# Key tiles cleared first, ScalarE's first operations chained, and the first projections reordered by kinds of parts

## The chip, the cores and the metric

The kernel runs on one core of one Trainium2 chip. The time is device microseconds (us) of that core for one execution, and smaller is better. A core has five engines with a queue of instructions each, worked off in order: PE (TensorE, matrix products and transposes), ACT (ScalarE), DVE (VectorE), POOL (GpSimd) and SP (SyncE, which here only issues DMAs). An instruction waits at the head of its queue until what it depends on is done, and everything behind it on that engine waits too.

## The reference

One layer of a hybrid decoder over 1024 tokens with 16 meta tokens put in front (1040 rows, model width 1024), all in float32:

```
u = RMSNorm(h)
z = u @ W_in -> [q | k | v | x_rec | y_rec]          (512 + 128 + 128 + 512 + 512 columns)
group A: causal depthwise conv(4) -> RG-LRU on x_rec, gated by GeLU(y_rec)
group B: sliding-window (128) attention, 8 heads on 2 KV heads, one sink per head
h += RMSNorm(concat(B_out, A_out) @ W_out)
h += RMSNorm(W2 relu(W1 RMSNorm(h))^2)
```

The output is h without the 16 meta rows. What the change touches lies in the first three lines: the norm of the input rows and the first products with W_in.

## The kernel before

**Products in three parts.** Every large product is done with operands split into a high part (the value cast to `float32r`) and a low part (the value less its high part). ACT makes the high part, then DVE subtracts to make the low part. `mm3` issues three matmuls per block of 128 of the contraction: high x high, high x low, low x high, into one PSUM accumulation (lines 108, 109, 110; the first operand is the weight).

**The head of the kernel.** The 1040 rows are worked in four chunks, `ALL = [(0, 272), (272, 256), (528, 256), (784, 256)]`. Chunk 0 holds the 16 meta rows and the x tiles 0 and 1; chunk b holds the x tiles 2b and 2b+1. For each chunk:

- `normed(b)` normalizes the rows. In `norm_rows`, ACT squares a tile and sums along the row (line 185), POOL adds epsilon and takes the power -0.5 (lines 143 and 149), and DVE multiplies the tile by the result (line 187).
- `transposed(b, xn)` transposes the normalized tile in eight column blocks kc = 0 to 7 on PE (line 227) into PSUM banks that rotate over three tags of two banks each. `split_scaled` evicts each block: ACT writes the high part `uh` with the gain (line 101), DVE the low part `ul` (line 102). The bank is free after the DVE step.
- Then four projections of the chunk, each with 128 columns of W_in: K, V, the first pair of Q heads, and the first x_rec chunk X. `project` runs over kc and calls `mm3` for each, so the three parts of one kc follow one another. The result is in a PSUM bank with the tag `acc`, of which there are two.
- A sink empties the bank. `sink_k` goes through `put_k`: for each of two heads ACT copies the high part to `khh` (line 288), DVE copies it to the other half (line 289) and subtracts to make `kl` (line 290). `sink_v` and the sink of X are one ACT copy each (lines 306 and 324); the sink of Q is `split_scaled` on two halves (lines 101 and 102).

**Weights.** `fetch` loads the columns of K, V, Q and X on the SP queue, between the loads of x. `split_w` splits them: an ACT cast (line 95) and a DVE subtraction (line 98). In the program text the splits of K and V (`wk`, `wv`) come ahead of `transposed(0, xn)`, those of Q and X (`wq`, `wx`) behind it. The unused halves of the two `kl` tiles are cleared on POOL (line 283); the text allocates them after the weight splits.

**What sets the order.** The kernel is written as one program of tiles with named slots (`bufs = {"raw": 2, "ws": 4, "a": 16, "b": 17, "c": 8, "d": 4, "e": 2}`). At build time a planner plays the program through on a simulated timeline, takes ready instructions by priority (the order of the text, unless `deferred` lowers it), gives out slots as they come free, and so fixes the order of each engine's queue and of the DMA issues. Waits are put in afterwards. A manual dependency of the class `NoSync` fixes an order on one engine for the planner and adds no wait on the chip. Because every queue's order comes out of that one play-through, a change in the head can also alter orders far behind it.

**Behind the head** stand the attention with the remaining projections filled in between, the recurrence, the output projection with its norms, and the two feed-forward products by a seven-product scheme over 2 x 2 blocks. `combine` (line 774) forms the sums of blocks there, and `w1_load` (line 771) issues the loads of W1.

Of the kernel before, what the change touches and what calls it, by code (L numbers as in the profile page):

```python
# [10 lines left out]
F32R = mybir.dt.float32r  # L11
AF = mybir.ActivationFunctionType
ALU = mybir.AluOpType
# [3 lines left out]
P = 128  # L17
D = 1024
KC = D // P
T = 1024  # L20
NMETA = 16
TT = T + NMETA
HD = 64
# [14 lines left out]
def hybrid_layer(  # L38
# [6 lines left out]
    nc = tc.nc  # L45
# [12 lines left out]
    def slot(tag, shape, dt=F32):  # L58
        uid[0] += 1
        return slab.tile(shape, dt, tag=tag, name=f"{tag}{uid[0]}", bufs=bufs[tag])  # L60

    def pair(tag, shape):
        return slot(tag, shape, F32R), slot(tag, shape, F32R)

    def bank(tag, shape=(P, 512)):
        uid[0] += 1
        return ps.tile(list(shape), F32, tag=tag, name=f"ps_{tag}{uid[0]}")

    def f32(ap):
        return ap.bitcast(F32)  # L70
# [22 lines left out]
    def split(hi, lo, src, eng=None):  # L93
        if eng is None:
            nc.scalar.copy(hi, src)  # L95
        else:
            eng.tensor_copy(hi, src)
        nc.vector.tensor_tensor(lo, src, f32(hi), op=ALU.subtract)  # L98

    def split_scaled(hi, lo, src, scale):  # L100
        nc.scalar.activation(hi, src, AF.Copy, scale=scale)
        nc.vector.scalar_tensor_tensor(
            lo, src, scale, f32(hi), op0=ALU.mult, op1=ALU.subtract
        )

    def mm3(dst, lhs, rhs, start, stop):
        (lh, ll), (rh, rl) = lhs, rhs
        nc.tensor.matmul(dst, lh, rh, start=start, stop=False, skip_group_check=True)  # L108
        nc.tensor.matmul(dst, lh, rl, start=False, stop=False, skip_group_check=True)  # L109
        nc.tensor.matmul(dst, ll, rh, start=False, stop=stop, skip_group_check=True)  # L110
# [68 lines left out]
    u = [pair("a", [P, TT]) for _ in range(KC)]  # L179
    RMS_SC = 1.0 / math.sqrt(D)  # L180

    def norm_rows(src, n):
        xn = slot("d", [P, D])
        ssq = small.tile([P, 1], F32, name="ssq", tag="ssq")
        nc.scalar.activation(xn[:n], src, AF.Square, scale=RMS_SC, accum_out=ssq[:n])
        rs = rstd_of([ssq[:n]], n)
        nc.vector.tensor_scalar(xn[:n], src, rs, None, op0=ALU.mult)
        return xn

    def project(w, pieces, sink):  # L190
        wh, wl = w
        for t0, n in pieces:
            acc = bank("acc")
            for kc in range(KC):
                uh, ul = u[kc]
                mm3(
                    acc[:, :n], (wh[:, kc, :], wl[:, kc, :]),
                    (uh[:, t0 : t0 + n], ul[:, t0 : t0 + n]),
                    kc == 0, kc == KC - 1,
                )  # L200
            sink(acc[:, :n], t0, n)

    ALL = [(0, 272), (272, 256), (528, 256), (784, 256)]
    REAL2 = [(16, 512), (528, 512)]

    zero = slot("ws", [P, 512])
    nc.vector.memset(zero, 0.0)
# [7 lines left out]
    def normed(b):  # L215
        rows = [(meta_t, NMETA)] if b == 0 else []
        rows += [(xt[2 * b], P), (xt[2 * b + 1], P)]
        return [(norm_rows(s[:m], m), m) for s, m in rows]

    def transposed(b, xn):  # L220
        t0, n = ALL[b]
        for kc in range(KC):
            flip[0] += 1
            pt = bank(("pt", "o", "s")[flip[0] % 3])
            o = 0
            for s, m in xn:
                nc.tensor.transpose(
                    pt[:, o : o + m], s[:m, kc * P : (kc + 1) * P], ident[:m, :m]
                )
                o += m  # L230
            uh, ul = u[kc]
            split_scaled(
                uh[:, t0 : t0 + n], ul[:, t0 : t0 + n], pt[:, :n],
                g_mix_col[:, kc : kc + 1],
            )

    def fetch(cols, tag="raw"):
        raw = slot(tag, [P, KC, P])
        o = 0
        for lo, n in cols:  # L240
            nc.sync.dma_start(
                raw[:, :, o : o + n],
                w_in[:, lo : lo + n].rearrange("(k p) c -> p k c", p=P),
            )
# [12 lines left out]
    load_x(2)  # L257
    load_x(3)
    rx = fetch([(X_COL, P)], "e")
    for i in range(4, 8):  # L260
        load_x(i)
    wk = split_w(rk, "b")
    wv = split_w(rv, "b")
    transposed(0, xn)
    wq = split_w(rq)
    wx = split_w(rx)
    nsink = const.tile([P, 8], F32, name="nsink")
    nc.sync.dma_start(nsink, attn_sinks[0].partition_broadcast(P))
    prm_r = slot("d", [8, 512])
# [10 lines left out]
    HALF = (slice(0, HD), slice(HD, P))  # L280
    vt = slot("c", [P, TT])
    for h in range(2):
        nc.gpsimd.memset(f32(kl[h][HALF[1 - h]]), 0.0)

    def put_k(hh, lo, src):
        for h in range(2):
            r, o = HALF[h], HALF[1 - h]
            nc.scalar.copy(hh[h][r], src[r])
# [19 lines left out]
    def new_q():  # L308
# [31 lines left out]
    prm = const.tile([P, NLRU, 8], F32, name="prm")  # L340
# [130 lines left out]
    def attend(j, half, sn):  # L471
        flat = [t_.rearrange("p a b -> p (a b)") for t_ in sn]
        for h in range(2):
# [28 lines left out]

            r, o = HALF[h], HALF[1 - h]
            part, whole = flat[h][r, 0:512], flat[0][r, 512:1024]
# [23 lines left out]
    def fill_q(j):  # L528
        def run(w):
            q, sink = new_q()  # L530
            project(w, REAL2, sink)
            qs[j] = q
        return run

    def fill_x(c):
        def run(w):
            xr, sink = new_x()
            project(w, ALL, sink)
            conv(c, xr, "b" if c == 3 else "d")
        return run  # L540

    def fill_y(c):
        def run(w):
# [4 lines left out]

            project(w, REAL2, sink)
            ys[c] = y  # L550
# [220 lines left out]
        nc.sync.dma_start(dst, w1v[b][:, :, c0 + P * a0 : c0 + P * a1])  # L771

    def combine(dst, x0, x1, op):
        nc.vector.tensor_tensor(dst, x0, x1, op=op)  # L774

    def operand(tiles):
        pairs = []
# [414 lines left out]
```

## Time and profile before

| | us |
|---|---|
| median of 3 runs | 1005.96 (1004.11 to 1006.33) |
| the profiled execution, whole | 996.57 |
| its span, first to last instruction | 994.6 |
| PE busy in the span | 960.6 |
| DVE busy | 672.4 |
| ACT busy | 505.0 |
| POOL busy | 76.3 |

A row of the timeline reads: start in us, duration in us, engine, line of the kernel, operation, what it writes, an arrow, what it reads, the shape, the count, and in square brackets how long the engine had been idle before it and which instruction ended that wait. Neighbouring rows of one engine overlap by the depth of its pipeline, so the step from one start to the next is what an instruction costs in a dense stretch. In the rows of waits stand the waiting engine, tile and line, what it waited for, and then the total, the number of times and the longest in us.

### The profile page before, as it was taken

The page shows a single profiled execution, that of the slowest core. Times are in us where ns is not written, and L with a number is a line of the kernel's source. Part 1 is how long each engine was busy: PE and PEld are TensorE (multiplying, and loading weights), DVE is VectorE, ACT ScalarE, POOL GpSimd, SP SyncE. Part 2 cuts the span into 40 slices and gives each one's busy share as a digit, 9 for nine tenths or more (in the row PEclk, how much of TensorE's full clock was granted, in tenths as well). Part 3 has the DMA queues.
Part 4 walks back from the last instruction along what each step waited for, and adds up shares of the span by engine and source line. Part 5 has one row for each costly group of instructions (what it writes and reads, how often), then busy time and mean ns, then how long its engine had stood idle before and what let it go on. Part 6 is the DMA issues. An engine that isn't in the chain of part 4 may idle for free.

```text
span 994.6 us, 12411 instructions
## 1 busy us (share of the span) xinstructions
PE 960.6 (97%) x4734; PEld 803.0 (81%) x4734; DVE 672.4 (68%) x995; ACT 505.0 (51%) x813; POOL 76.3 (8%) x108
## 2 busy tenths in 40 slices
PE   6999999999999979999999989999999999999996
PEld 6999999888788867778888868888888888888775
DVE  6679996756956685564654455458566676779965
ACT  7557573658735553343555656555443344444522
POOL 4000000000012100000000000000121100002031
PEclk9999999999999989999999999999999999999999
DMA  8101001112146345576532264222778765547582
GB/s 280 32 16 49 23 22 43 43 43 64 43 148 211 121 134 171 189 241 224 171 125 86 85 212 127 86 105 85 190 170 183 198 221 180 191 169 203 157 228 89
DMA packets 89371, 133.28 MB, mean 134 GB/s; under 512 B 13752, under 2 KB 52680, under 8 KB 89312
## 3 DMA queue, kind: packets, MB, share of 16 engines
q1 hardware_dynamic: 80704, 110.47, 33.1%
q0 software_dynamic: 8320, 20.97, 9.8%
q10 hardware_dynamic: 288, 1.05, 0.3%
q8 instruction: 37, 0.61, 0.2%
q14 instruction: 22, 0.18, 0.1%
HBM read 113.60 MB, written 18.87 MB: 133 GB/s over the span
## 4 chain that ended last, share of the span: by engine, by line
PE 81%; DVE 6%; DMA 6%; issue 3%; ACT 2%; POOL 1%; SPq 0%; POOLq 0%; DVEq 0%; ACTq 0%
PE ps_acc L109 10%; PE ps_acc L108 10%; PE ps_acc L110 10%; PE ps_pt L109 6%; PE ps_pt L110 6%; PE ps_pt L108 6%; PE ps_s L108 5%; PE ps_s L109 5%; PE ps_s L110 5%; PE ps_o L110 5%; PE ps_o L109 5%; PE ps_o L108 5%; DMA raw<-in_w_ff_dram 3%; PE ps_o L491 2%; PE ps_pt L480 1%
## 5 line engine op out<-in xcount | busy, mean ns | idle before, releaser
L95 ACT CAST ws<-raw 128x1024 fp32r<-128x1024 f32 (+1 forms) x70 | 71.7, 1024 | 116.1 <-PE ps_o L109 54.6
L98 DVE TENSOR_TENSOR ws<-raw,ws 128x1024 fp32r<-128x1024 f32 (+1 forms) x71 | 84.6, 1192 | 45.4 <-ACT ws L95 45.4
L108 PE MATMUL ps_acc<-a,ws 128*128 128x256 f32 (+2 forms) x272 | 90.5, 333 | 0.6 <-DVE b L290 0.6
L109 PE MATMUL ps_acc<-a,ws 128*128 128x256 f32 (+2 forms) x272 | 89.8, 330 | 0.0
L110 PE MATMUL ps_acc<-a,ws 128*128 128x256 f32 (+2 forms) x272 | 89.4, 329 | 0.0
L95 ACT CAST ws<-e 128x1024 fp32r<-128x1024 f32 x44 | 46.1, 1048 | 74.8 <-PE ps_o L109 42.7
L98 DVE TENSOR_TENSOR b<-b,b 128x1024 fp32r<-128x1024 f32 (+2 forms) x48 | 57.6, 1199 | 32.3 <-PE ps_o L109 24.6
L98 DVE TENSOR_TENSOR ws<-e,ws 128x1024 fp32r<-128x1024 f32 x44 | 53.8, 1222 | 24.8 <-ACT ws L95 24.8
L95 ACT CAST b<-b 128x1024 fp32r<-128x1024 f32 (+2 forms) x48 | 49.4, 1030 | 40.1 <-DVE b L774 38.0
L149 POOL TENSOR_TENSOR rs<-ms,half_pow 128x1 f32<-128x1 f32 (+1 forms) x33 | 28.3, 861 | 384.6 <-DVE ms L145 383.2
L108 PEld LDWEIGHTS ps_acc<-a,ws 128*128 128x128 f32 x272 | 51.2, 188 | 4.9 <-DVE b L290 0.8
L110 PEld LDWEIGHTS ps_acc<-a,ws 128*128 128x128 f32 x272 | 51.2, 188 | 4.6
L109 PEld LDWEIGHTS ps_acc<-a,ws 128*128 128x128 f32 x272 | 51.2, 188 | 3.9
L109 PE MATMUL ps_acc<-ws,b 128*128 128x512 f32 x110 | 43.6, 396 | 2.0 <-DVE ws L98 2.0
L109 PE MATMUL ps_pt<-ws,b 128*128 128x512 f32 x112 | 44.4, 396 | 0.0
L108 PE MATMUL ps_pt<-ws,b 128*128 128x512 f32 x112 | 44.1, 394 | 0.0
L110 PE MATMUL ps_pt<-ws,b 128*128 128x512 f32 x112 | 44.1, 394 | 0.0
L108 PE MATMUL ps_s<-ws,b 128*128 128x512 f32 x110 | 43.8, 398 | 0.0
L110 PE MATMUL ps_s<-ws,b 128*128 128x512 f32 x110 | 43.7, 397 | 0.0
L109 PE MATMUL ps_s<-ws,b 128*128 128x512 f32 x110 | 43.6, 396 | 0.0
L110 PE MATMUL ps_acc<-ws,b 128*128 128x512 f32 x110 | 43.5, 396 | 0.0
L108 PE MATMUL ps_acc<-ws,b 128*128 128x512 f32 x110 | 43.5, 395 | 0.0
(368 smaller groups left out, 2669.6 us busy)
## 6 DMA issues: line engine op xcount, KB each, us to landing
raw<-in_w_ff_dram SPq DMA_DIRECT2D x64, 512.0 KB, 4.1
e<-in_w_ff_dram SPq DMA_DIRECT2D x44, 512.0 KB, 3.5
d<-in_w_ff_dram SPq DMA_DIRECT2D x16, 512.0 KB, 5.3
s_dram<-d POOLq DMA_DIRECT2D x16, 512.0 KB, 4.0
raw<-in_w_ff_dram POOLq DMA_DIRECT2D x12, 512.0 KB, 5.5
raw<-in_w_in_dram SPq DMA_DIRECT2D x9, 512.0 KB, 3.7
c<-in_x_dram SPq DMA_DIRECT2D x8, 512.0 KB, 9.0
d<-in_x_dram SPq DMA_DIRECT2D x8, 512.0 KB, 5.3
```

Source lines behind the costliest of these rows:

```text
L95: nc.scalar.copy(hi, src)
L98: nc.vector.tensor_tensor(lo, src, f32(hi), op=ALU.subtract)
L108: nc.tensor.matmul(dst, lh, rh, start=start, stop=False, skip_group_check=True)
L109: nc.tensor.matmul(dst, lh, rl, start=False, stop=False, skip_group_check=True)
L110: nc.tensor.matmul(dst, ll, rh, start=False, stop=stop, skip_group_check=True)
L149: nc.gpsimd.tensor_tensor(rs[:n], ms[:n], half_pow[:n], op=ALU.pow)
L480: nc.tensor.transpose(pt[:, o : o + P], sn[h][:, 2 * bp + i, s * P : (s + 1) * P], ident,)
L491: nc.tensor.matmul(po[:, oc : oc + n], v, p_[:, pc : pc + n], start=first and k == 0, stop=last and k == 1, skip_group_check=True,)
```

## The change

Three things are changed in the head of the kernel; the number of matmuls, transposes, splits and DMAs stays the same.

1. `khh` and `kl` are allocated, and the two halves of `kl` cleared on POOL, before the first tiles of the norm rather than after the weight splits.
2. ScalarE's first operations are chained by order-only dependencies in this order: the cast of K's weights, the eight `uh` evictions of chunk 0, the cast of V's weights, the Square of x tile 2, the cast of Q's weights, the Square of x tile 3, the cast of X's weights. To that end the split of V's weights stands behind `transposed(0, xn)` in the text, and the norms of x tiles 2 and 3 stand between the weight splits (in the old text `normed(1)` stands behind all four splits and behind the loads of `nsink` and of the parameters `prm_r`).
3. For the four first projections in each chunk, `project` gives way to `project_by_parts`: one kind of part over all eight kc, then the next kind. K runs high x high, then low weights x `uh`, then high weights x `ul` (`late_u`); V, Q and X run high x high, then high weights x `ul`, then low weights x `uh` (`late_w`).

`split` and `combine` now return an instruction or note its name in `mark`; nothing in the changed text uses either. The later projections keep `project`.

```diff
-        nc.vector.tensor_tensor(lo, src, f32(hi), op=ALU.subtract)
+        low = nc.vector.tensor_tensor(lo, src, f32(hi), op=ALU.subtract).ins
+        mark[0] = low.name
+        return low
+    mark = [None]
+
+    def behind(name, *inss):
+        for ins in inss:
+            tc.add_manual_dep(
+                ins, name,
+                mybir.DependencyInfo(
+                    mybir.DependencyClass.NoSync, mybir.DependencyReason.DATA
+                ),
+                reason="order",
+            )
...
     def split_scaled(hi, lo, src, scale):
-        nc.scalar.activation(hi, src, AF.Copy, scale=scale)
+        high = nc.scalar.activation(hi, src, AF.Copy, scale=scale).ins
...
+        return high
...
-    def norm_rows(src, n):
+    def norm_rows(src, n, link=False):
...
+        if link:
+            chained(ins)
...
+    def project_by_parts(w, piece, sink, order):
+        t0, n = piece
+        acc = bank("acc")
+        for i, (a, b) in enumerate(order):
+            for kc in range(KC):
+                nc.tensor.matmul(
+                    acc[:, :n], w[a][:, kc, :], u[kc][b][:, t0 : t0 + n],
+                    start=i == 0 and kc == 0, stop=i == 2 and kc == KC - 1,
+                    skip_group_check=True,
+                )
+        sink(acc[:, :n], t0, n)
...
+    khh = [slot("b", [P, T], F32R) for _ in range(2)]
+    kl = [slot("b", [P, T], F32R) for _ in range(2)]
+    HALF = (slice(0, HD), slice(HD, P))
+    for h in range(2):
+        nc.gpsimd.memset(f32(kl[h][HALF[1 - h]]), 0.0)
...
+    last_act = [None]
+
+    def chained(ins):
+        if last_act[0] is not None:
+            behind(last_act[0], ins)
+        last_act[0] = ins.name
+
+    def split_w_chained(raw, tag="ws"):
+        hi, lo = pair(tag, [P, KC, P])
+        chained(nc.scalar.copy(hi, raw).ins)
+        nc.vector.tensor_tensor(lo, raw, f32(hi), op=ALU.subtract)
+        return hi, lo
...
-            split_scaled(
+            high = split_scaled(
...
+            if b == 0:
+                chained(high)
...
-    wk = split_w(rk, "b")
-    wv = split_w(rv, "b")
+    wk = split_w_chained(rk, "b")
     transposed(0, xn)
-    wq = split_w(rq)
-    wx = split_w(rx)
+    wv = split_w_chained(rv, "b")
+    xn = [(norm_rows(xt[2], P, True), P)]
+    wq = split_w_chained(rq)
+    xn.append((norm_rows(xt[3], P, True), P))
+    wx = split_w_chained(rx)
...
-    khh = [slot("b", [P, T], F32R) for _ in range(2)]
-    kl = [slot("b", [P, T], F32R) for _ in range(2)]
...
-    for h in range(2):
-        nc.gpsimd.memset(f32(kl[h][HALF[1 - h]]), 0.0)
...
-            transposed(b, normed(b))
-        piece = [ALL[b]]
-        project(wk, piece, sink_k)
-        project(wv, piece, sink_v)
-        project(wq, piece if b else [(16, 256)], sink_q0)
-        project(wx, piece, sink_x0)
+            transposed(b, xn if b == 1 else normed(b))
+        late_u, late_w = ((0, 0), (1, 0), (0, 1)), ((0, 0), (0, 1), (1, 0))
+        project_by_parts(wk, ALL[b], sink_k, late_u)
+        project_by_parts(wv, ALL[b], sink_v, late_w)
+        project_by_parts(wq, ALL[b] if b else (16, 256), sink_q0, late_w)
+        project_by_parts(wx, ALL[b], sink_x0, late_w)
```

More of the change, by code (lines that the diff above doesn't have):

```diff
@@ L180, in hybrid_layer @@
     RMS_SC = 1.0 / math.sqrt(D)
-    def norm_rows(src, n):
+    def norm_rows(src, n, link=False):
         xn = slot("d", [P, D])
         ssq = small.tile([P, 1], F32, name="ssq", tag="ssq")
-        nc.scalar.activation(xn[:n], src, AF.Square, scale=RMS_SC, accum_out=ssq[:n])
+        ins = nc.scalar.activation(
+            xn[:n], src, AF.Square, scale=RMS_SC, accum_out=ssq[:n]
+        ).ins
+        if link:
+            chained(ins)
         rs = rstd_of([ssq[:n]], n)
@@ L272, in hybrid_layer @@
         nc.sync.dma_start(prm_r[4 + i : 5 + i, :], src)
-    khh = [slot("b", [P, T], F32R) for _ in range(2)]
-    kl = [slot("b", [P, T], F32R) for _ in range(2)]
     vk = [slot("b", [P, 8, P], F32R) for _ in range(2)]
-    HALF = (slice(0, HD), slice(HD, P))
     vt = slot("c", [P, TT])
-    for h in range(2):
-        nc.gpsimd.memset(f32(kl[h][HALF[1 - h]]), 0.0)
     def put_k(hh, lo, src):
@@ L773, in combine @@
     def combine(dst, x0, x1, op):
-        nc.vector.tensor_tensor(dst, x0, x1, op=op)
+        return nc.vector.tensor_tensor(dst, x0, x1, op=op).ins
     def operand(tiles):
```

## The prediction

> **What bounds the kernel now.** I read the page first: busy time, then the chain that ended last.
>
> ```profile
> span 994.6 us, 12411 instructions
> PE 960.6 (97%) x4734; PEld 803.0 (81%) x4734; DVE 672.4 (68%) x995; ACT 505.0 (51%) x813; POOL 76.3 (8%) x108
> PE 81%; DVE 6%; DMA 6%; issue 3%; ACT 2%; POOL 1%; SPq 0%; POOLq 0%; DVEq 0%; ACTq 0%
> ```
>
> PE is the bound: busy 97%, and 81% of the chain. A change that leaves the count of matmuls alone can only win where PE stands still or runs slowly. The change lies in the first 50 us, so the next views are the windows there and PE's waits, up to 30 us and then from 27.6 to 140 us.
>
> ```profile
> 6.10:11.20 5.10, 3.66 (x19) 2.90 (x18) 3.80 (x5) 3.61 (x6) 3.79 (x6) 1.00 1.17 317
> 11.20:18.20 7.00, 6.50 (x29) 5.80 (x27) 6.17 (x11) 6.33 (x14) 2.11 (x5) 1.00 1.02 374
> 18.20:27.60 9.40, 8.83 (x74) 8.57 (x73) 7.49 (x19) 6.39 (x17) 2.09 (x3) 1.00 0.77 226
> 27.60:51.00 23.40, 23.40 (x198) 23.23 (x198) 14.35 (x35) 13.12 (x34) 2.48 (x6) 1.00 0.02 5
> ...
> PE ps_o L227 <- DVE d L187: 1.3, 2, 0.7
> PE ps_acc L108 <- DVE b L290: 0.6, 1, 0.6
> PE ps_o L227 <- DVE a L102: 0.5, 1, 0.5
> ```
>
> The columns of a window are its length and the busy time of PE, weight loads, DVE, ACT and POOL. After 27.60 PE is busy 23.40 of 23.40 us; chunks 1 to 3 can therefore gain nothing. Before it there are three waits: for the normalized x tile 1 (`d`, L187), for a bank that the eviction of a low part frees (`a`, L102), and for a bank that the sink of chunk 0's K frees (`b`, L290). The fourth loss is in PE's timeline: its matmuls step slowly at first. The chain of the head has one row per matmul; the other rows are PE's own.
>
> ```profile
> 9.91 0.47 PE L227 MATMUL ps_o<-ident,d 128*128 128x128 f32 x1 [0.75 <-DVE d L187]
> 11.27 0.82 PE L108 MATMUL ps_acc<-a,b 128*128 128x272 f32 x2
> 12.58 0.90 PE L227 MATMUL ps_o<-ident,d 16*128 16x16 f32 x3 [0.50 <-DVE a L102]
> ...
> 13.49 0.23 PE ps_acc L109
> ...
> 14.62 0.23 PE ps_acc L108
> 14.85 0.83 PE ps_s L227 x3
> 15.68 0.23 PE ps_acc L109
> ...
> 18.17 0.23 PE ps_acc L108
> 18.40 0.14 PE ps_acc L109
> 18.54 0.12 PE ps_acc L110
> ...
> 21.63 0.29 PE L110 MATMUL ps_acc<-a,b 128*128 128x272 f32 x1
> 27.58 0.39 PE L108 MATMUL ps_acc<-a,ws 128*128 128x272 f32 x1 [0.57 <-DVE b L290]
> ```
>
> K and V of chunk 0 are 48 matmuls of 272 columns. Two start at 11.27, six run from 13.49 to 14.85, and the remaining 40 fill 15.68 to about 21.76. Up to 18.40 one costs 0.23 us, after it 0.125: the same work at half speed, though the windows give a granted clock of 1.00 throughout, so here the matmul's step is the measure of the clock.
>
> **The change part by part.** First the rows of ACT, DVE and POOL around the start.
>
> ```profile
> 8.30 1.04 ACT L95 CAST b<-raw 128x1024 fp32r<-128x1024 f32 x1 [1.04 <-DMA raw<-in_w_in_dram]
> 9.78 1.05 ACT L95 CAST b<-raw 128x1024 fp32r<-128x1024 f32 x1 [0.44 <-DMA raw<-in_w_in_dram]
> 10.73 0.48 ACT L101 ACTIVATE a<-ps_o,gcol 128x272 fp32r<-128x272 f32 x1
> 11.11 0.48 ACT L101 ACTIVATE a<-ps_s,gcol 128x272 fp32r<-128x272 f32 x1
> 15.10 1.06 ACT L185 ACTIVATE d<-c 128x1024 f32<-128x1024 f32 x1 [0.67 <-PE ps_s L227]
> 21.45 0.17 ACT L288 CAST km<-ps_acc 64x16 fp32r<-64x16 f32 x1 [1.81 <-PE ps_acc L110]
> ...
> 6.81 0.75 DVE L187 TENSOR_SCALAR d<-c,rs 128x1024 f32<-128x1024 f32 x1
> 8.33 1.52 DVE L187 TENSOR_SCALAR d<-c,rs 128x1024 f32<-128x1024 f32 x1 [0.77 <-POOL rs L149]
> 9.77 2.34 DVE L98 TENSOR_TENSOR b<-raw,b 128x1024 fp32r<-128x1024 f32 x2
> 12.04 0.49 DVE L102 SCALAR_TENSOR_TENSOR a<-ps_o,gcol,a 128x272 fp32r<-128x272 f32 x1
> 12.45 0.48 DVE L102 SCALAR_TENSOR_TENSOR a<-ps_s,gcol,a 128x272 fp32r<-128x272 f32 x1
> ...
> 2.73 0.19 POOL L363 TENSOR_SCALAR_AFFINE_SELECT mask<-mask 128x16 f32<-128x16 f32 x1
> 4.11 0.23 POOL L143 TENSOR_SCALAR ms<-ssq 16x1 f32<-16x1 f32 x1 [1.19 <-ACT d L185]
> 7.72 0.57 POOL L149 TENSOR_TENSOR rs<-ms,half_pow 128x1 f32<-128x1 f32 x1
> 8.35 2.38 POOL L283 MEMSET b<- 64x1024 f32 x2
> ```
>
> *The key tiles' clearing.* The same DVE multiply takes 0.75 us for x tile 0 and 1.52 for x tile 1, and beside the second POOL runs the two clearings (8.35 to 10.73). With these gone the second should take 0.75 too, and PE's wait of 0.75 before 9.91 goes: transposes of tile 1 at 9.14. Cost of the clearing's new place: POOL is idle from 2.92 to 4.11, and all 2.38 us put in there hold the meta rows' L143 until 5.30. Its chain of about 0.9 us then ends at 6.2, some 0.3 us after tile 0's was to begin (its POOL work comes between the meta rows' and tile 1's, which still starts at 7.34). So the cost is 0 to 0.3 us on tile 0, whose transposes PE finishes long before 9.14; I take 0.
>
> *ScalarE's order.* The cast of V's weights at 9.78 leaves the front; ACT is free at 9.34. Block 0's transposes end at 9.14 + 0.47 = 9.61, its `uh` starts at 9.65 instead of 10.73 and ends at 10.1, where PE's first product starts instead of at 11.27: 1.1 us earlier. On DVE one weight subtraction (half of 2.34) stands ahead of the `ul` evictions instead of two, and starts at 9.4 instead of 9.77: `ul` 0 starts at 10.6 instead of 12.04, and its bank is free at 11.1. Blocks 6 and 7 wait for that bank and the next (0.41 later), so their transposes run at 11.1 and 11.5 or soon after. ACT's eight evictions step by 0.38 (10.73, 11.11): 9.65 + 5 x 0.38 = 11.55 for block 5, then 11.9 and 12.3 for 6 and 7, the last ending at 12.8.
>
> *Kinds of parts in chunk 0.* K's eight high x high products need `uh` alone. From 10.1 PE has 8 x 0.23 = 1.8 us of these and 0.90 + 0.83 = 1.7 us of transposes: 3.5 us by addition, with ACT's last eviction at 12.8 the lower bound plus one product (13.0). I take 13.3 with 40 products left. Before, 40 were left at 15.68. So PE is 2.4 us ahead here, all of it time in which a product costs 0.23. K's second kind needs the low weights (10.6), its third the `ul`, of which the last comes at 10.6 + 8 x 0.41 = 13.9: before PE gets there (13.3 + 8 x 0.23 = 15.1). V needs its weights: cast 12.8 to 13.9 on ACT, subtraction to 15.1 on DVE, and PE comes to V at 16.9 or, at full speed, not before 15.3. Hidden.
>
> *The clock.* What the 2.4 us are worth depends on when the step falls to 0.125. Stays it at 18.40: 5.1 / 0.23 = 22 products by then, 18 x 0.125 = 2.2, end at 20.6, gain 1.2 us. Moves it with the first product (1.1 earlier): 4.0 / 0.23 = 17, 23 x 0.125 = 2.9, end at 20.2, gain 1.6. Moves it with the end of PE's last gap (2.4 earlier): gain 2.4. The trace has one such switch and does not tell these apart. I take 2.0, between the last two, because the switch came 5.2 us after PE became gapless (13.2) and that moment moves most; the ends 1.2 and 2.4 stay in the range.
>
> *The bank of K.* K and V were interleaved before (`ps_acc` L108 x2 at 11.27), both ended at about 21.4, and K's sink freed its bank only 6.1 us later, at 27.5. With K's products first in one row, K ends at 16.9 or sooner, and with the same 6.1 us its bank is free at 23.0; X wants it at 27.0 - 2.0 = 25.0. The wait of 0.6 goes. What is late next is chunk 1's norm: the Square of tile 2 found its data at 15.10 at the latest (it waited for PE, not for a DMA). In the chain the cast of Q, the Square of tile 3 and the cast of X follow, about 1.05 us each: Square 3 ends by 18.3 (before: 17.66), then POOL's 1.1 us and DVE's 0.75 give the tile at 20.1. PE gets there at 21.76 - 2.0 = 19.8: 0 to 0.8 us lost, I take 0.2. Q's weights are split by 18.5, X's by 20.6, both ahead of need. All SP loads keep their order; only `prm_r` takes its slot after tile 3's norm, and no PE work before 50 us needs it.
>
> *Chunks 1 to 3.* By kinds, a projection asks for all `uh` at once and `ul` or low weights later. PE is gapless there and no other wait of it occurs up to 140 us, so the inputs lie ready: 0 us. Without that cover each missing block would cost one eviction, 0.38 to 0.41 us. Every matmul loads its weights in either order (4734 and 4734 in the page), so no load is saved.
>
> **Sum.** 2.0 + 0.6 - 0.2 = 2.4 us. After 27.6 us PE paces everything, so I carry it to the end. On the profiled execution: 996.57 - 2.4 = 994.2 us. The median of the runs shown is 9.4 us above that execution, which the change has no part in: 1005.96 - 2.4 = 1003.6 us.
>
> **The rivals.** *The clock doesn't follow.* The switch stays where it is: 1.2 + 0.6 - 0.2 = 1.6 us, 1004.4. For it speaks that nothing in the trace ties the switch to the first product; against, that it came only after PE was gapless for 5 us. [...]
>
> *The clearing doesn't move.* If the planner still gives POOL the two clearings at 8.35, tile 1's multiply ends at 9.85 as now, every step above comes some 0.7 us later, and 2.4 - 0.7 = 1.7 remains: 1004.3. The text's place alone doesn't bind POOL's order; against it, the masks of a later line (L363) ran at 2.73, so POOL takes what is ready.
>
> *The orders behind the head come out differently, and a weight load is late.* This is the case on the slower side. The longest wait of PE behind the head:
>
> ```profile
> PE ps_acc L109 <- DVE b L98: 5.8, 1, 5.8
> ...
> 352.61 7.64 DMA raw<-in_w_ff_dram
> ...
> 352.61 4.38 SPq L771 DMA_DIRECT2D raw<-in_w_ff_dram  x2
> ```
>
> PE stood 5.8 us because DVE's sums of W1 blocks waited for loads issued from 352.61. If the new play-through puts one more such pair ahead on SP, the wait grows by 4.4 us: 1003.6 + 4.4 = 1008.0. It decides once the delay exceeds 2.4 us. Against it: these loads start as buffers come free behind PE's own work, so they should shift with the head. The same place can also shrink: one pair less is 999.2.
>
> **How the numbers follow.** Forecast as summed (1.8 to 3.2 us gained): 0.47. Clock stays: 0.15. Clearing stays: 0.08. Later orders, slower: 0.20; later orders, quicker: 0.10. The range reaches from 1000.6, between the forecast's best (1002.8) and 999.2, to 1007.4, nearly the slow case; the likeliest's own range is 1002.8 to 1004.2. About 0.2%, 2.0 us or 1003.9, is what a measurement can tell here. Faster: 0.35 of the forecast's 0.47 (it straddles the bound), and 0.10: 0.45. Slower: of the slow case's 0.20 most, 0.18. The rest, 0.37, is within.
>
> **What would show it.** DVE's second L187 takes 0.75 and PE's wait before it is gone; first `ps_acc` product at about 10.1; K's last at about 17, V's at 19.4 to 20.6; no wait of PE on `b` L290 near 25; the next Q product 2 us earlier. Wrong it would be if PE waited on ACT's chain for tile 3 or Q's weights, if the switch to 0.125 came no earlier, or if PE's waits behind 140 us, the 5.8 us above all, added up to another sum.

## The result, and the profile after

The changed kernel is slower, by 0.6%. Its median is 1010.56 us (1008.63 to 1012.28, six runs) against 1003.88 us (1003.39 to 1006.33, six runs) of the kernel before beside it: a ratio of 1.0061, with a 95% interval of 1.0043 to 1.0079. The forecast was 1003.6 us, 2.4 below the 1005.96 from which it started. The profiled execution of the changed kernel took 1010.26 us, its span 1008.3 us.

The page of the changed kernel, the three lines that answer to those shown of before:

```profile
span 1008.3 us, 12411 instructions
PE 966.0 (96%) x4734; PEld 805.6 (80%) x4734; DVE 675.0 (67%) x995; ACT 504.5 (50%) x813; POOL 77.2 (8%) x108
PE 68%; DVE 10%; DMA 9%; issue 8%; ACT 3%; POOL 2%; SPq 0%; POOLq 0%; DVEq 0%; ACTq 0%
```

The counts of instructions are the same. PE is busy 5.4 us longer (966.0 for 960.6) at a mean granted clock of 0.985 for 0.991, so with equal counts part of its work ran more slowly. In the chain that ended last PE's share fell from 81% to 68%. Not all of this is the change: a second profile of the kernel before (e1 below) has PE busy for 961.7 us, a clock of 0.990 and a share of 72%.

The head is where the forecast looked. PE's timeline in the changed kernel, one row for each stretch that matters:

```profile
11.06 0.90 PE L229 MATMUL ps_acc<-a,b 128*128 128x272 f32 x2
13.88 6.88 PE L229 MATMUL ps_acc<-a,b 128*128 128x272 f32 x45
...
22.48 3.10 PE L229 MATMUL ps_acc<-a,ws 128*128 128x256 f32 x24
...
27.83 0.33 PE L282 MATMUL ps_pt<-ident,d 128*128 128x128 f32 x1 [0.94 <-DVE a L117]
...
29.14 0.33 PE L282 MATMUL ps_s<-ident,d 128*128 128x128 f32 x1 [0.54 <-DVE d L207]
...
30.09 4.61 PE L229 MATMUL ps_acc<-a,ws 128*128 128x272 f32 x24
```

The 48 products of K and V end at 20.76 us; before they ended at 21.92. Q follows at 22.48, 0.5 us earlier than before. Then X, which used to start at 27.58, starts only at 30.09, and its 24 products take 4.6 us (3.1 before). Between Q and X stand 16 transposes (4 of chunk 1 and 12 of chunk 2), with stops for the norm of a tile of chunk 2. The windows around that place say why X then ran slowly; the columns are as in the prediction, and the third number from the end is the granted clock:

```profile
26.60:30.00 3.40, 1.81 (x9) 1.07 (x9) 3.18 (x7) 3.35 (x9) 1.69 (x4) 0.95 0.53 133
30.00:33.00 3.00, 3.00 (x15) 2.91 (x14) 2.94 (x8) 2.95 (x7) 0.00 (x0) 0.50 0.02 5
33.00:36.00 3.00, 3.00 (x26) 3.00 (x26) 1.89 (x8) 1.55 (x4) 0.00 (x0) 0.99 0.00 0
```

PE did 15 instructions in 3 us at a granted clock of 0.50, and 26 in the next 3 us. In the stretch ahead of them, from 26.60 to 30.00, it was busy for 1.81 of 3.40 us, with transposes alone. What held X's bank is seen on DVE and ACT. Rows of POOL, DVE and ACT in the changed kernel; the first two groups are the clearing, the Square and the power of x tile 0 and the multiply of x tile 1, the others the sink of chunk 0's K:

```profile
1.02 2.11 POOL L245 MEMSET b<- 64x1024 f32 x2
5.37 1.06 ACT L201 ACTIVATE d<-c 128x1024 f32<-128x1024 f32 x1 [1.40 <-DMA c<-in_x_dram]
6.92 0.57 POOL L165 TENSOR_TENSOR rs<-ms,half_pow 128x1 f32<-128x1 f32 x1
...
9.05 0.76 DVE L207 TENSOR_SCALAR d<-c,rs 128x1024 f32<-128x1024 f32 x1 [0.77 <-POOL rs L165]
...
18.62 0.15 ACT L340 CAST km<-ps_acc 64x16 fp32r<-64x16 f32 x1
24.37 0.37 ACT L340 CAST b<-ps_acc 64x256 fp32r<-64x256 f32 x1
27.60 1.05 ACT L201 ACTIVATE d<-c 128x1024 f32<-128x1024 f32 x1
28.77 0.37 ACT L340 CAST b<-ps_acc 64x256 fp32r<-64x256 f32 x1
...
26.54 0.42 DVE L341 CAST b<-ps_acc 64x256 fp32r<-64x256 f32 x1
29.61 0.43 DVE L342 TENSOR_TENSOR b<-ps_acc,b 64x256 fp32r<-64x256 f32 x1
```

The same in the kernel before: the Square and the power of x tile 0, then the sink's last steps on ACT and DVE:

```profile
4.64 1.06 ACT L185 ACTIVATE d<-c 128x1024 f32<-128x1024 f32 x1 [0.62 <-DMA c<-in_x_dram]
6.20 0.57 POOL L149 TENSOR_TENSOR rs<-ms,half_pow 128x1 f32<-128x1 f32 x1
...
25.88 0.37 ACT L288 CAST b<-ps_acc 64x256 fp32r<-64x256 f32 x1 [0.63 <-DVE b L290]
...
27.10 0.43 DVE L290 TENSOR_TENSOR b<-ps_acc,b 64x256 fp32r<-64x256 f32 x1
```

K is ready earlier than before (its first sink step runs at 18.62), and yet its sink ends at 30.04 rather than at 27.5. On ACT the first large copy stands behind six evictions of chunk 1, the second behind the Squares of two tiles of chunk 2 (the last at 27.60); on DVE the first step (26.54) stands behind the low-part evictions of chunk 1. So two things end together at 30.04 to 30.09: PE's queue reaches X, and X's bank comes free.

The head explains less than half of the loss. Four landmarks, in us (the copy of chunk 0's X, the last attention part of line 505 or 557, the start of the last Square of the second feed-forward half of line 1088 or 1140, and the span). "Before, again" is a second profiled execution of the kernel before (1005.16 us), since the first, at 996.57, lay 7 us under the median:

| | X copied | attention ends | last Square | span | span after last Square |
|---|---|---|---|---|---|
| before | 30.9 | 217.1 | 941.5 | 994.6 | 53.1 |
| before, again | 31.9 | 218.1 | 949.9 | 1003.2 | 53.3 |
| after | 34.7 | 220.2 | 951.3 | 1008.3 | 57.0 |

Against the second execution of before the changed kernel loses 2.1 us up to the attention's end, gains 0.7 in the 730 us behind that, and loses 3.7 us behind the last Square. The end is 700 us away from the edit. There the order of the queues has changed. SP's last weight loads in the kernel before, again, and then in the changed kernel:

```profile
962.97 0.37 SPq L1014 DMA_DIRECT2D e<-in_w_ff_dram  x1
964.11 0.37 SPq L1014 DMA_DIRECT2D raw<-in_w_ff_dram  x1
...
970.67 0.74 SPq L1014 DMA_DIRECT2D raw<-in_w_ff_dram  x1
```

```profile
964.37 0.37 SPq L1066 DMA_DIRECT2D raw<-in_w_ff_dram  x1
...
972.37 0.74 SPq L1066 DMA_DIRECT2D e<-in_w_ff_dram  x1
973.20 0.48 SPq L1066 DMA_DIRECT2D raw<-in_w_ff_dram  x1
```

One load of `e` has moved behind an output store and another load, and the last issue comes 2.5 us later; the last Square is already late by 1.4 of these. On DVE the order of the last row tiles has changed too. The last steps on DVE in the kernel before, again (L1097 is the sum of a row tile, L1102 its two output steps):

```profile
990.67 1.42 DVE L1102 SCALAR_TENSOR_TENSOR a<-a,rs,d 128x512 f32<-128x512 f32 x2 [0.46 <-POOL rs L149]
...
992.68 0.69 DVE L1097 TENSOR_TENSOR a<-ps_pt,a 128x512 f32<-128x512 f32 x1
993.28 1.41 DVE L1102 SCALAR_TENSOR_TENSOR a<-a,rs,d 128x512 f32<-128x512 f32 x2
...
995.27 0.69 DVE L1097 TENSOR_TENSOR a<-ps_o,a 128x512 f32<-128x512 f32 x1
...
998.39 1.42 DVE L1102 SCALAR_TENSOR_TENSOR a<-a,rs,d 128x512 f32<-128x512 f32 x2 [0.44 <-POOL rs L149]
```

And in the changed kernel (L1149 and L1154 are the same two lines):

```profile
992.91 1.41 DVE L1154 SCALAR_TENSOR_TENSOR a<-a,rs,d 128x512 f32<-128x512 f32 x2 [0.46 <-POOL rs L165]
...
995.44 1.42 DVE L1154 SCALAR_TENSOR_TENSOR a<-a,rs,d 128x512 f32<-128x512 f32 x2 [0.44 <-POOL rs L165]
996.77 0.69 DVE L1149 TENSOR_TENSOR a<-ps_pt,a 128x512 f32<-128x512 f32 x1
...
999.45 1.41 DVE L1154 SCALAR_TENSOR_TENSOR a<-a,rs,d 128x512 f32<-128x512 f32 x2 [0.44 <-POOL rs L165]
1000.78 0.68 DVE L1149 TENSOR_TENSOR a<-ps_o,a 128x512 f32<-128x512 f32 x1
...
1003.51 1.41 DVE L1154 SCALAR_TENSOR_TENSOR a<-a,rs,d 128x512 f32<-128x512 f32 x2 [0.44 <-POOL rs L165]
```

Before, the sum of a tile ran ahead of the output steps of the tile before it, so that its Square on ACT and its root on POOL lay beside those steps. After, the sums of the last two tiles stand behind the output steps, and every tile pays the chain over ACT, POOL and DVE by itself: from the first output step to the last 7.7 us before, 10.6 us after.

### The profile page after: what moved, and what is told of

The parts are those of the page before. It is cut to its first block, busy times and chain, and to the rows that moved or that the text cites. A ratio compares the mean times of both kernels' runs of the same rounds, so it can differ in the third digit from the quotient of the medians.

```text
span 1008.3 us, 12411 instructions
## 1 busy us (share of the span) xinstructions
PE 966.0 (96%) x4734; PEld 805.6 (80%) x4734; DVE 675.0 (67%) x995; ACT 504.5 (50%) x813; POOL 77.2 (8%) x108
## 3 DMA queue, kind: packets, MB, share of 16 engines
q0 software_dynamic: 8320, 20.97, 10.1%
## 4 chain that ended last, share of the span: by engine, by line
PE 68%; DVE 10%; DMA 9%; issue 8%; ACT 3%; POOL 2%; SPq 0%; POOLq 0%; DVEq 0%; ACTq 0%
PE ps_acc L125 7%; PE ps_acc L124 7%; PE ps_acc L126 7%; PE ps_pt L125 5%; PE ps_pt L126 5%; PE ps_pt L124 5%; PE ps_acc L229 4%; PE ps_s L126 4%; PE ps_s L125 4%; PE ps_s L124 4%; DMA raw<-in_w_ff_dram 4%; PE ps_o L125 4%; PE ps_o L124 4%; PE ps_o L126 4%; DMA e<-in_w_ff_dram 2%
## 5 line engine op out<-in xcount | busy, mean ns | idle before, releaser
L95 ACT CAST ws<-e 128x1024 fp32r<-128x1024 f32 x42 | 43.9, 1046 | 74.4 <-PE ps_o L125 24.3
L98 DVE TENSOR_TENSOR b<-b,b 128x1024 fp32r<-128x1024 f32 (+2 forms) x48 | 57.6, 1200 | 27.3 <-PE ps_o L125 19.6
L124 PE MATMUL ps_acc<-a,ws 128*128 128x512 f32 (+2 forms) x208 | 72.3, 348 | 0.0
L125 PE MATMUL ps_acc<-a,ws 128*128 128x512 f32 (+2 forms) x208 | 71.6, 344 | 0.0
L126 PE MATMUL ps_acc<-a,ws 128*128 128x512 f32 (+2 forms) x208 | 71.5, 345 | 0.0
L98 DVE TENSOR_TENSOR ws<-e,ws 128x1024 fp32r<-128x1024 f32 x42 | 51.4, 1223 | 22.9 <-ACT ws L95 22.9
L125 PE MATMUL ps_pt<-b,ws 128*128 128x512 f32 x104 | 41.5, 399 | 1.4 <-DMA b<-t_dram 1.4
L126 PEld LDWEIGHTS ps_acc<-a,ws 128*128 128x128 f32 x208 | 39.1, 188 | 4.6
L126 PE MATMUL ps_o<-ws,b 128*128 128x512 f32 x108 | 42.5, 394 | 0.0
```

Source lines behind the costliest of these rows:

```text
L98: low = nc.vector.tensor_tensor(lo, src, f32(hi), op=ALU.subtract).ins
```

## The experiments

All ratios are to the kernel before, run beside on the same chip; its median there was 1002.88 us for e1 to e4, 1002.98 for e5 to e8, 997.03 for e9 to e11 and 1003.12 for e12.

**e1: the kernel before, again.** Nothing is edited.

> The kernel before, unchanged, for a second profile. The profiled execution shown of before took 996.6 us, the median of its runs 1003.9. If the head is fixed by the orders of the queues, X of chunk 0 ends at about 30.7 us here too, and the products of the second feed-forward half begin at the same place; if an execution of about 1004 us is the usual one, the 7 us more stand in PE's waits for weight loads behind 700 us, and the comparison of the two first traces overstates what the change costs there.

Measured: 1005.16 us in one run. Its profile is the yardstick above. It has waits of PE on late weight splits that end at 800, 954 and 981 us; the first profile had these shorter or not at all (the longest, 2.0 us, ends at 946). So the difference between the first profile of before and that of the changed kernel overstates the change.

**e2: the clearing alone.** The kernel before, with `khh`, `kl` and the clearing moved to the front.

```diff
+    khh = [slot("b", [P, T], F32R) for _ in range(2)]
+    kl = [slot("b", [P, T], F32R) for _ in range(2)]
+    HALF = (slice(0, HD), slice(HD, P))
+    for h in range(2):
+        nc.gpsimd.memset(f32(kl[h][HALF[1 - h]]), 0.0)
+
     zero = slot("ws", [P, 512])
```

> Only the key tiles' clearing is moved ahead; the orders of PE and SP are those of before. Theory A (the loss comes from changed orders of the queues): no loss, 0 to 0.8 us quicker, since tile 1's multiply takes 0.75 instead of 1.52 us. Theory B (the early clearing delays the meta rows and tile 0, and with them the loads' consumers): 0.5 to 2 us slower. Under both the head ends within 1 us of before.

Measured: 1003.8 us, ratio 1.0005 (0.9989 to 1.0021). The clearing alone is worth nothing that can be measured, and PE's and SP's orders stay those of before.

**e3: ScalarE's chain alone.** The changed kernel with the clearing put back and `project` for the four projections.

```diff
-        project_by_parts(wk, ALL[b], sink_k, late_u)
...
+        piece = [ALL[b]]
+        project(wk, piece, sink_k)
```

> Only ScalarE's fixed order, with the old projections and the old place of the clearing. Theory A: PE's queue has all 16 transposes of chunks 1 and 2 between Q and X of chunk 0, as in the changed kernel; X of chunk 0 ends at about 34.5 us instead of 30.7, the granted clock falls to 0.5 for about 3 us, and the kernel is 3 us slower from the head alone, 5 to 6 if the order of the last weight loads (also changed here) costs as well. Theory C (the kinds of parts cost the time): within 1 us of before.

Measured: 1010.83 us, ratio 1.0086 (1.0062 to 1.0111). The chain by itself brings the whole loss, head and end. PE's timeline there:

```profile
30.30 0.59 PE L124 MATMUL ps_acc<-a,ws 128*128 128x272 f32 x1
30.69 0.43 PE L125 MATMUL ps_acc<-a,ws 128*128 128x272 f32 x1
30.91 0.43 PE L126 MATMUL ps_acc<-a,ws 128*128 128x272 f32 x1
```

X starts at 30.30 and steps by 0.23 us, as in the changed kernel, and the landmarks are 35.0, 220.8 and 950.7 us, with 57.9 us behind the last.

**e4: the kinds of parts alone.** The kernel before with `project_by_parts` for the four projections.

```diff
-        project(wk, piece, sink_k)
...
+        project_by_parts(wk, ALL[b], sink_k, late_u)
```

> Only the projections by kinds of parts. PE's queue keeps 7 or 8 transposes ahead of X of chunk 0, so theory A expects a head as long as before or up to 1 us shorter; the order of the last weight loads on SP is the changed one here, so 2 to 3 us slower in all if that order costs, and -1 to 0 us if it does not. Theory C (the kinds of parts cost the time): 3 us or more slower, seen before 60 us.

Measured: 1012.58 us, ratio 1.0098 (1.0076 to 1.0121). PE's waits up to 60 us, and X:

```profile
PE ps_acc L208 <- ACT a L101: 1.9, 2, 1.0
PE ps_acc L208 <- DVE b L302: 1.6, 1, 1.6
...
32.49 3.27 PE L208 MATMUL ps_acc<-a,ws 128*128 128x272 f32 x24 [1.55 <-DVE b L302]
```

Without ScalarE's order the high x high products outrun the `uh` evictions (two waits of 0.9 to 1.0 us), the granted clock is 0.54 from 16.5 to 23 us, and X starts at 32.49. This is more than theory A allowed for, and it is seen before 60 us, as theory C said (X copied at 35.8, attention ends at 222.3). So the kinds need the chain, but neither costs nothing by itself. Since e3 and e4 end in the same new order (57.9 and 58.0 us behind the last Square), two theories were left for the head (PE's order, K's bank) and one for the end.

**e5: PE's order in the head.** The changed kernel, with the transposes of chunk 2 behind X of chunk 0 on PE. Along with it all queues end in the order of before.

```diff
+                if b == 2:
+                    behind(last_x[0], tr)
...
+        mm = project_by_parts(wx, ALL[b], sink_x0, late_w)
+        if b == 0:
+            last_x[0] = mm.name
```

> The changed kernel, but the transposes of chunk 2 stand behind the last product of X of chunk 0 on PE (order alone, no wait). DVE's order at the end of the program is then that of the kernel before too. Theory 1 (PE's own order is the loss of the head: 12 transposes of chunk 2 stand ahead of X of chunk 0 and wait for tile 5's norm): X of chunk 0 starts at 27.5 or sooner and its 24 products take 3.1 us, not 4.45; the kernel ends at 1002 to 1004, level with the one before. Theory 2 (K's bank, freed only at 30.04 by its sink, is the loss by itself): X still starts at 30 or later, and only the tail's share comes back, some 3 us: 1006 to 1008. Theory 3 (what is lost is neither head nor tail): 1009 to 1011.

Measured: 1007.52 us, ratio 1.0045 (1.0029 to 1.0062). PE's timeline and two windows:

```profile
29.85 5.50 PE L229 MATMUL ps_acc<-a,ws 128*128 128x272 f32 x24 [4.08 <-DVE b L346]
```

```profile
29.85:33.00 3.15, 3.15 (x14) 3.15 (x15) 1.96 (x7) 1.43 (x2) 0.00 (x0) 0.50 0.02 5
33.00:36.00 3.00, 3.00 (x20) 3.00 (x20) 0.00 (x0) 0.61 (x2) 0.00 (x0) 0.69 0.00 0
```

PE reaches X early and stands 4.08 us for K's bank. That decides for the bank: PE's order alone was not the loss, and the bank by itself is enough to hold X. The head is even 1.9 us worse than in the changed kernel (attention ends at 222.1), because the transposes no longer fill the wait and the slow stretch is longer (a clock of 0.69 from 33 to 36 us, where the changed kernel has 0.99). The end is back to 55.0 us, still 1.5 us above the longest of the other profiles with the old order of all queues; why is not known.

**e6: K's sink first.** The changed kernel, with the evictions of chunk 1 behind the sink of chunk 0's K on ACT and DVE.

```diff
+        if after:
+            behind(after[0], high)
+            behind(after[1], low)
...
-            nc.scalar.copy(hh[h][r], src[r])
+            k_act[0] = nc.scalar.copy(hh[h][r], src[r]).ins.name
```

> The changed kernel, but the evictions of chunk 1 stand behind K's sink of chunk 0 on ScalarE and VectorE, so K's bank is free earlier. The order at the end of the program stays that of the changed kernel. Theory 1 (PE's order alone): K's bank is free by 27, but the transposes ahead of X still wait for tile 5, X starts near 30; 1009 to 1011. Theory 2 (K's bank): X starts at 27 or sooner, X's last product by 30.5 instead of 34.7; the head's loss of about 3 us comes back, the tail's stays: 1006 to 1008. If both bind at one moment, neither this kernel nor the one before it gains by itself.

Measured: 1008.57 us, ratio 1.0056 (1.0034 to 1.0077). PE's X and the last step of the sink:

```profile
25.20 3.25 PE L232 MATMUL ps_acc<-a,ws 128*128 128x272 f32 x24 [0.88 <-DVE b L347]
...
24.63 0.43 DVE L347 TENSOR_TENSOR b<-ps_acc,b 64x256 fp32r<-64x256 f32 x1
```

X starts at 25.20 and runs at full speed. The landmarks are 28.5, 217.9 and 948.2 us: the head's loss is gone, and the end is still 58.3 us. Two limits of this run: in the new play-through the transposes of chunk 2 also come behind X, as in e5, so the bank and PE's order changed together, and what PE's order costs with the bank free early was not run. And the whole time, 1.0056, is not clear of the changed kernel's 1.0061 and 0.6 us above what theory 2 foretold; that the head is repaired is read from the landmarks.

The start of this profile bears on the clock. PE's first three products of K, the two rows together, stand behind twelve transposes of full size:

```profile
11.02 0.72 PE L232 MATMUL ps_acc<-a,b 128*128 128x272 f32 x2
...
12.08 0.37 PE L232 MATMUL ps_acc<-a,b 128*128 128x272 f32 x1
```

The third product takes 0.37 us where the changed kernel's took 0.57, so the full rate was there at 12.08, when PE had done two products in all and transposes for most of the 3 us ahead of them.

**e7: DVE's order at the end, repaired.** The changed kernel, with the output steps of a tile behind the sum of the next.

```diff
+            if j < 3:
+                behind(half[j + 1][1], stt)
...
+        finish_sum(j, accs[j])
+        if j:
+            finish_out(j - 1)
+    finish_out(3)
```

> The changed kernel, but at its end the output steps (L1154) of row tile j-1 stand behind the sum (L1149) of tile j on VectorE, as in the kernel before. Nothing ahead of 980 us differs. Theory T (the end's 3 us come from VectorE's order there: the sums of tiles 2 and 3 wait behind output steps, so that the chains over ScalarE, GpSimd and VectorE run one after the other): the last four sums lie within about 8 us instead of 10.6, and the kernel is 2 to 3 us quicker than the changed one: 1007.5 to 1008.5. Rival U (the end's loss comes from loads and out store moved on SP, or PE's last products being later): sums' spread may fall, but the time stays 1009.5 to 1011.

Measured: 1009.44 us, ratio 1.0057 (1.0036 to 1.0077), 1.1 us under the changed kernel's median. Theory T is half right at most: the last four output steps spread over 9.4 us instead of 10.6, and behind the last Square stand 56.9 us instead of 57.0. The rest is PE:

```profile
994.82 0.69 DVE L1151 TENSOR_TENSOR a<-ps_pt,a 128x512 f32<-128x512 f32 x1
...
998.97 0.69 DVE L1151 TENSOR_TENSOR a<-ps_o,a 128x512 f32<-128x512 f32 x1 [1.48 <-PE ps_o L126]
```

Now the sum of the last tile waits for PE, whose products end later too. In the changed kernel 66 of PE's instructions come after the cast of the late weight block, in the kernel before, again, 59.

**e8: DVE's order at the end, broken.** The kernel before, with the sums of the last two tiles behind the output steps of the tile ahead.

```diff
+        add = nc.vector.tensor_tensor(acc[:, c], y, acc[:, c], op=ALU.add).ins
+        if j > 1:
+            tc.add_manual_dep(
+                add, last_out[0],
```

> The kernel before, with VectorE's order at its end made that of the changed kernel: the sums of row tiles 2 and 3 stand behind the output steps of the tile ahead. The head, PE's and SP's orders are as before. Theory T: 2 to 3 us slower than the kernel before, about 1005 to 1006. Rival U: level with it, 1002 to 1004.

Measured: 1005.69 us, ratio 1.0030 (1.0015 to 1.0044). DVE's order by itself costs 2.7 us, and 57.6 us stand behind the last Square, as many as with the whole new end; e7 shows that undoing it alone doesn't give that back once PE's products are late as well.

**e9: K's sink first, and the old end.** On the kernel of e6:

```diff
+                if (j, half, k) == (0, 0, 3):
+                    nc.scalar.activation(
+                        sn[h][:, k, 0:256], sn[h][:, k, 0:256], AF.Copy,
+                        scale=rden[:, h, k : k + 1],
+                    )
+                    continue
```

> The kernel with K's sink first (e6), and in the first attention step (j 0, half 0) the last of the four normalizing multiplies of each head goes to ScalarE. That edit is worth nothing in itself (two operations of 0.35 us), but with it all queues end in the order of the kernel before. So the head is that of e6, the end that of the kernel before. Theory H+E (what the change loses is the head's bank plus the end's order, and nothing else): level with the kernel before, 1002 to 1004, some 5 us quicker than e6. Theory G (PE paces everything behind 28 us, so that e6's lead of 2.5 us there is kept): 1000 to 1001. Rival R (a loss that neither head nor end explains): 1006 or more.

The edit moves one multiply of the first attention step to ACT, for each of two heads; with it all queues end in the order of before.

Measured: 996.98 us against 997.03, ratio 1.0002 (0.9988 to 1.0016). With the head's bank and the end's order repaired nothing of the loss is left: theory H+E holds, R is out. The changed kernel itself was not run on this chip, on which the kernel before is 6 us quicker than on the others, so no time shows that its loss would appear there too. The landmarks speak for it: the end takes 53.5 us here, and 57.0 to 58.3 in the profiles with the new end. Theory G is out too. X is copied at 29.2 us, 1.7 to 2.9 us ahead of the six profiles without the chain and the kinds, and attention ends at 217.5, where it does before (217.1 to 218.5).

**e10 and e11: DVE relieved in the attention,** on e9 and on the kernel before.

```diff
+                if k in (3,):
+                    nc.scalar.activation(
```

> As e9, but that multiply goes to ScalarE in all eight attention steps: 16 operations of 0.35 us, 5.6 us of VectorE's work between 76 and 180 us, where it is busy 93%. The end's order is that of the kernel before. Theory V (VectorE, nearly full there, eats a lead of the head): PE's lead over the kernel before, 2 us at 60 us, is still 1.5 to 2 us at 180 us, and the kernel is 1 to 2 us quicker than e9. Rival L (the lead is lost to latencies of the attention chain, or ScalarE's longer queue): no quicker than e9.

> The kernel before with the same 16 multiplies on ScalarE; its end's order is unchanged. Theory V: PE is gapless from 28 to 220 us in the kernel before, so relief of VectorE is worth nothing by itself: 1002 to 1004, level. Rival L: if ScalarE's longer queue delays the attention chain, 1004 or more; if VectorE's load held PE back all along in steps that are too short to see, 1001 or less.

Measured: 997.42 us, ratio 1.0002 (0.9993 to 1.0012), and 997.09 us, ratio 1.0001 (0.9990 to 1.0012). Theory V falls: the lead is lost with a relieved DVE as well. It is lost at one place. The windows of e10 and then of e11:

```profile
152.00:156.00 4.00, 3.50 (x28) 3.04 (x26) 3.04 (x4) 2.70 (x6) 0.00 (x0) 1.00 0.02 4
```

```profile
152.00:156.00 4.00, 4.00 (x37) 4.00 (x36) 3.80 (x4) 0.69 (x2) 0.00 (x0) 1.00 0.14 40
```

In these 4 us PE does 28 instructions against 37. Its queue there holds only transposes of probabilities and value products, with stops between them (busy 3.50 of 4.00 us), where the kernel before has products of projections between them. Why the planner left none is not settled.

**e12: the new end on the old head.** The kernel before, with the first and the last of the four normalizing multiplies on ACT in all attention steps; with this edit all queues end as in the changed kernel.

```diff
+                if k in (0, 3):
+                    nc.scalar.activation(
```

> The kernel before, with two of the four normalizing multiplies of every attention step (the first and the last) on ScalarE: the last alone was worth nothing (e11), and PE's work to 220 us should end where it did, within 0.5 us. But with this edit all queues end in the order of the changed kernel. Theory E (that order is the larger part of the loss, by itself and whatever the head does): 3.6 to 5 us slower than the kernel before, ratio 1.0036 to 1.005. Rival H (the head is the larger part, and the end costs what e8 showed or less): ratio 1.000 to 1.003.

Measured: 1008.33 us, ratio 1.0049 (1.0031 to 1.0067). The edit isn't quite free in itself: attention ends at 219.8 us, 1.3 us behind e11. The end takes 58.0 us. So of the 5.2 us some 1.3 are the edit's and some 4 the order's.

**The sum.** Behind the last Square the five profiles with the new end (after, e3, e4, e6, e12) take 57.0 to 58.3 us, six with the old end (both of before, e2, e9, e10, e11) 52.3 to 53.5. That is about 4 to 5 us. Between them lies e5 (55.0, old end); e7 and e8, with DVE's order alone repaired or broken, take 56.9 and 57.6. The head costs 2.1 us at the end of the attention. Together this is about the 6.7 us measured (5.1 between the two spans of the table), and e9 has neither. None of the twelve beats the kernel before: repaired in both places, the change comes out level with it.

## Why the prediction was wrong

- **The clearing** moved, and DVE's multiply of x tile 1 fell from 1.52 to 0.76 us, as said. The first product came at 11.06 (10.85 to 11.27 in six profiles with the whole change) and not at 10.1, for two reasons. In the changed kernel's profile the loads landed later: the Square of x tile 0 starts at 5.37 for 4.64, waiting for its DMA, and POOL's power for it follows 1.55 us behind, as in the kernel before (6.92 and 6.20). This lateness is no effect of the clearing. But where the loads land early, the new place isn't free: in e9 and e10 that Square starts at 4.75 and 4.45 and the power only at 6.74 and 6.71, because POOL works off the masks behind the clearing (until 6.31 in e10). The multiply of x tile 1 starts 1.52 us behind that of x tile 0 in both kernels, so lateness of tile 0 is handed on. The cost on tile 0, put at 0 to 0.3 us and taken as 0, was 0.4 to 0.7 us there, and no profile reaches 10.1.
- **Kinds of parts and the clock** were right in direction, if too small. K and V ended at 18.94 to 20.76 us in those six profiles and at 21.92 to 23.17 in the six without the chain and the kinds: 2.8 us earlier on average, for 2.0 foretold. Products came to the full rate (a step of 0.125 us for 0.23) at 16.1 us in the changed kernel and by 12.1 to 14.8 in the five others with the whole change, at 17.3 to 20.0 in the six without. That the switch moves was the right choice; where it falls is not settled by the first product's start: six profiles whose products start within 0.4 us have it between 12.1 and 16.1.
- ***The bank of K* is the step that failed in the head.** That with the same 6.1 us its bank is free at 23.0 took the sink's length for a property of the sink. It is a place in two queues. K was ready sooner, at about 17.6 us (worked out: 45 products from 13.88 to 20.59, where the next transpose starts, fit with 0.23 us each up to 16.2 and 0.125 behind, and 21 of them are K's), but ACT and DVE took its sink behind chunk 1's evictions and chunk 2's Squares, and the bank came free at 30.04: 12.4 us. e5 shows that the bank alone is enough to hold X, e6 that X starts at 25.2, beside the foretold 25.0, when the sink goes first and chunk 2's transposes come behind X. Even there the bank comes free at 25.06 and not at 23.0, and PE waits 0.88 us for it.
- **The clock was counted only once.** With X late, 4.6 us pass without a product, and X runs at 0.50 for 3 us: 1.5 us more. Between 25.5 and 30.09 PE did 16 transposes and never stood still for over 0.94 us at once, but it was busy for only 1.81 of the 3.40 us from 26.60 on. What brought the clock down is not shown. The missing products alone need not have: in e6 the full rate was there at 12.08 us, after transposes and two products (0.37 us for a product, 0.57 in the changed kernel). So the idle half may as well be the cause, and no run parts the two. Nor does the longest stop ahead of X tell by itself: 4.08 us in e5 (0.50), 0.94 in the changed kernel (0.50), 0.88 in e6 (full rate).
- ***"After 27.6 us PE paces everything, so I carry it to the end"* is the other step that failed.** It fails twice. A lead of the head doesn't last: e9's is gone at 156 us, in an order of the attention's work that the trace of before couldn't show. And the end of the program got another order, for 4 to 5 us. That later orders could differ was a rival, with the right sign and a chance of 0.20; its place was wrong. The wait behind the loads of 352.61 us, 5.8 us before, was 5.9 us in the changed kernel and no part of the loss. The end of the program was the place that has no cover: every us there is a us of the total.
- The norm of chunk 1 (0 to 0.8 us, taken as 0.2) and the parts of chunks 1 to 3 (0) were right in size: PE waits 0.4 us for that norm, at 21.85, and between 36 and 140 us not at all in the changed kernel.

## What to carry to other kernels

Don't carry a wait's length over to a changed kernel: a sink that takes 6 us takes them because of what stands ahead of it in the queues, and the question is what stands there afterwards. Where one play-through sets all orders, an edit anywhere can re-sort a near-tie far away, so compare the queues' orders at the end of the program, where nothing hides a delay, before the head is credited with anything. When a part seems to cost or gain a few us, run it with the far order held equal (as e9 and e12 do) before that figure is believed.

## What the runs showed of the hardware that was not expected

- The granted clock fell to 0.50 without any long stop: from 29.66 to 33.08 us in the changed kernel, after a stretch at 1.00 (26.25 to 29.66) in which PE was busy for 1.68 us with transposes alone and stood still for 0.94 at the longest. In e5 and e4 the slow stretch was longer, by estimate about 6.9 and 6.8 us: the mean clocks are 0.79 (25.40 to 29.85), 0.50 (to 33.00) and 0.69 (to 36.00) in e5, 0.54 (16.50 to 23.00) and 0.86 (to 26.00) in e4, each taken as a mix of 0.50 and 1.00.
- The full rate can come after a stretch of transposes: in e6 it was there at 12.08 us, after twelve of full size and two products; that third product took 0.37 us, in the changed kernel 0.57 (at 12.82).
- The windows give a clock of 1.00 for the slow start, though a product that starts a row takes 0.57 us there and 0.37 at the full rate; the step of the products (0.23 or 0.125 us) tells the rate.
- The kernel before has medians from 997.03 (one chip) to 1003.88 us (1002.88 to 1003.88 in the four other sets), and its two profiles differ by 8.6 us in span. 1.0 us of that lies ahead of the attention's end, 7.4 between it and the last Square and 0.2 behind it. One profile of before is no base for a forecast to 0.2%.
- The first loads don't land at a fixed time: the cast of K's weights, which waits for its DMA, started between 8.30 and 10.00 us in the fourteen profiles.
